# Attention's score, turn and value steps in other places, two more units turned by DMA, and two changes of order at norms

## The chip, the cores and the metric

The kernel runs on one core of one Trainium2 chip. The time is the device time of one execution in microseconds; the number that counts is the median of several runs. PE is the engine of the matmuls, DVE the vector engine, ACT the scalar engine, POOL the GpSimd engine, and SP the engine whose queue issues most DMAs.

## The reference

Two layers over 512 tokens of width 1024, all in float32. Each layer is a feed-forward block, a mixing block and a second feed-forward block; a norm ends the whole.

```python
for l in range(DEPTH):
    x = x + 0.5 * swiglu(rms_norm(x, ffn1_norm[l]), ffn1_wg[l], ffn1_wu[l], ffn1_wd[l])
    h = rms_norm(x, mix_norm[l])
    z = h @ w_in[l]            # q 512 | k 128 | v 128 | conv_B 512 | conv_C 512 | conv_h 512
    attn_out = sliding_window_attention(q, k, v, attn_sink[l])
    conv_out = short_conv(conv_B, conv_C, conv_h, conv_w[l])
    x = x + concat([attn_out, conv_out]) @ w_out[l]
    x = x + 0.5 * swiglu(rms_norm(x, ffn2_norm[l]), ffn2_wg[l], ffn2_wu[l], ffn2_wd[l])
return rms_norm(x, final_norm)
```

Attention has eight query heads of 64 and two key heads (four query heads share one). A block of 128 queries sees its own block of keys and the one before it, masked to a window of 128, with a bias that grows with the distance, and with one learned sink per head in the softmax:

```python
m = max(scores.max(-1), sink)
p = where(mask, exp(scores - m), 0)
probs = p / (p.sum(-1) + exp(sink - m))
out = probs @ v_band
```

## The kernel before, in words

**Products in two parts.** Every float32 product is made of three PE matmuls in a rounded format: high part of the weights by high and by low part of the data, and low part of the weights by high part of the data. So each tile of weights that arrives (`raw`) is split: ACT casts the high part (`wh`, line 222), DVE subtracts it from the raw tile for the low part (`wl`, line 223). `need_split` makes the splits in the order of the plan, `take_split` hands the next one to a group of matmuls and asks for the split three groups ahead. `need_raw` asks for the loads four units further ahead, from SP's queue; some units are sums of two tiles, and the second is added by an accumulating DMA from POOL's queue. Raw tiles live in a ring of eight buffers (`stock`), high and low parts in rings of four.

**Order of the work.** The program's order says what depends on what; a planner then places the instructions on each engine, by its own estimate of when each is ready, and sets the waits. `tc.issue_after(a)` (also `behind`) keeps later instructions of an engine behind instruction `a` on it, without waiting for its end. Inside `manual_schedule` regions PE keeps the order of the program.

**The mixing block** (`mix`). The norm's result comes as turned halves; `halves` makes the first three groups from them (keys, values, first pair of query heads), with weights that `hold` takes ahead. Then groups of 24 matmuls follow, one per 128 columns of `w_in`: j = 1 to 3 for the other query heads, then twelve for the convolution (two of C, two of h, two of B, twice). After each of them `attend(step)` issues a piece of attention; steps 3 to 5 follow the query groups j = 1 to 3 and 6 to 17 the twelve others. In this document the group before `attend(step)` is called group `step`.

**Attention by units.** A unit is one block of queries and one key head with its four query heads: unit number 4 g + n for block n and key head g. Blocks n = 0 have one block of keys, the others two. Each unit has these pieces, and each piece has a table that gives the step for each of the eight units:

- `scores`: matmuls of scores, then DVE adds the bias and takes the maximum, ACT takes the exponentials (line 1565), DVE divides. The probabilities `p` lie in a buffer of the raw ring.
- the turn, which the values need with keys across partitions. Either on PE (`turn`): up to eight transposes of 128x128 (line 1623), then a cast on ACT and a subtraction on DVE for each block of keys (lines 1626, 1627). Or by DMA, for the units with an entry in `SEND_AT`: `apart` (called at the end of `scores`) copies the two 16-bit halves of each number into two planes with two ACT copies (line 1588), `send` turns each plane with one transposing DMA from SP's queue (line 1595), `join` puts the halves together again with two ACT copies (line 1608), and casts and subtracts as the other way does (lines 1612, 1614).
- `values`: matmuls of the turned probabilities with the values (lines 1638, 1639), a copy on ACT and two additions on DVE.

A join of `JOIN_AT` is issued in `attend` itself; one of `LATE_JOIN_AT` after the split that follows it in `go_on`.

**Norms behind closing groups.** In `share` with `after`, the last products of a block end in the residual stream `x`; `after` is the next norm. Its squares are taken on ACT as parts of `x` are ready, its factor is found by a first guess on ACT (`guess`, line 650) and a Newton step on DVE (lines 649 to 661), and the scaled tiles `xn` are turned on PE (line 685). Of a turned tile, ACT casts the high part, and `rest` (DVE subtraction for the low part, line 697) and `keep` (a full copy on ACT, line 701; nothing at a mixing norm) are collected in `later` and issued by `go_on`, each behind the instruction that is named beside it. `added` is the last addition to `x`, `first` the second scaled tile.

Of the kernel before, what the change touches and what calls it, by code (L numbers as in the profile page):

```python
# [16 lines left out]
P = 128  # L17
# [25 lines left out]
EARLY = ("a11", "a12", "s3", "s2", "a22", "s1", "s4")  # L43
SCORES_AT = (5, 6, 7, 8, 9, 10, 12, 13)
TURN_AT = (6, None, 8, None, 11, None, 14, 15)
SEND_AT = (None, 7, None, 9, None, 11, None, None)
JOIN_AT = (None, None, None, None, None, 14, None, None)
LATE_JOIN_AT = (None, 10, None, 12, None, None, None, None)
VALUES_AT = (7, 11, 9, 13, 12, 15, 15, 16)
WARM = 3  # L50
# [26 lines left out]
def trunk_kernel(  # L77
# [252 lines left out]
    def hold(norm, n):  # L330

        first = state["group"]
        if norm.added:
            for ahead, one in ((2, norm.added), (3, norm.first)):
                with behind(one):
                    need_split(first + ahead)
        return [take_split(SPLIT_AHEAD - j)[1:] for j in range(n)]

# [243 lines left out]
    class Norm:  # L582
# [40 lines left out]
        def __call__(self, t, o):  # L623

            self.squared = nc.scalar.activation(
                junk(f"sq_{self.i}_{t}_{o}"),
# [52 lines left out]
        def turn(self, t, o, xn):  # L679
# [23 lines left out]
            if self.later is None:  # L703
                rest()
                keep()
            elif o:
                self.later.extend(((rest, "added"), (keep, "squared")))
            else:
                rest()
                self.later.append((keep, "squared"))  # L710

# [240 lines left out]
    def share(  # L952
# [6 lines left out]
        for step, (acc, operand, start) in enumerate(chains):  # L959
# [9 lines left out]
            for h in range(2):  # L969
# [11 lines left out]
                for o, t, sign in shares[step]:  # L981
                    for m in range(2):
# [7 lines left out]
                        if after and step == 6 and m:  # L990
                            after.added = added
                            after.go_on()
            if not soon:
# [493 lines left out]
    def mix(l, norm, after):  # L1487
# [36 lines left out]
        class Unit:  # L1524
# [52 lines left out]
            def apart(self):  # L1577

                if n_of(self) % NT == 1:
                    self.room = g8(f"pr_{self.name}", U16, (P, 4, KC * P))  # L1580
                else:
                    self.room = xpool.tile(
                        [P, 4, KC * P], U16, tag="xf", bufs=8, name=f"pr_{self.name}"
                    )
                src = self.p.bitcast(U16).rearrange("p h (b k z) -> p z h b k", b=2, z=2)
                with tc.issue_after(state["cast"].ins):
                    for z in range(2):
                        nc.scalar.copy(
                            self.room[:, z].rearrange("p (b h k) -> p h b k", b=2, h=4), src[:, z]
                        )  # L1590

            def send(self):
                with tc.issue_after(state["load"].ins):
                    for z in range(2):
                        nc.sync.dma_start_transpose(
                            self.room[:, 2 + z].rearrange("p (g q) -> p g q", q=P), self.room[:, z]
                        )

            def join(self):

                dst = self.p.bitcast(U16).rearrange("p h (k z) -> p z (h k)", z=2)
                turned = self.p.rearrange("p h k -> p (h k)").rearrange(
                    "p (b h q) -> p b h q", b=2, h=4
                )
                self.pt = []
                with tc.issue_after(state["cast"].ins):
                    for z in range(2):
                        nc.scalar.copy(dst[:, z], self.room[:, 2 + z])
                for kb in range(2):
# [39 lines left out]

        def n_of(unit):  # L1650
            return NT * unit.g + unit.n

        def attend(step, what=(VALUES_AT, JOIN_AT, TURN_AT, SEND_AT, SCORES_AT)):

# [29 lines left out]
        def go_on():  # L1684
# [4 lines left out]
            with tc.issue_after(last.ins) if last else nullcontext():  # L1689
                need_split(state["group"] - 1 + SPLIT_AHEAD)  # L1690
            attend(step - 1, (LATE_JOIN_AT,))

# [75 lines left out]
```

## Time and profile before

| what | value |
|---|---|
| median of 3 runs | 1641.26 us (1640.89 to 1641.5) |
| profiled execution | 1641.66 us |
| its span, first to last instruction | 1639.9 us |
| mean granted PE clock | 0.999 |
| PE transposes `pt` of attention | 64, both layers |
| transposing DMAs of attention | 12, both layers |

All times in rows are of this one profiled execution, in microseconds from the start of its span. A matmul's row shows how long it was under way; PE starts the next one before it ends, so the distance between starts tells what an instruction costs PE. A row of busy time counts overlapping instructions once. "Idle before" is time in which that engine had nothing under way, with what ended it.

### The profile page before, as it was taken

How to read it: one execution, taken by the hardware profiler on the slowest of the kernel's cores; microseconds unless marked ns; L12 is line 12 of the kernel's file. 1: busy time of each engine (PE TensorE's matmuls, PEld its weight loads, DVE VectorE, ACT ScalarE, POOL GpSimd, SP SyncE). 2: the span in 40 equal slices, each digit the busy share in tenths (PEclk: the TensorE clock that was granted, in tenths of full speed). 3: DMA queues.
4: the chain of work that ended last, by engine and by line, in shares of the span. 5: the costliest groups of instructions: out<-in, count | busy, mean ns of one | idle time of the engine just before them, and what ended most of it. 6: DMA issues, size and time to landing. Idle time of an engine off the chain costs nothing.

```text
span 1639.9 us, 21080 instructions
## 1 busy us (share of the span) xinstructions
PE 1629.8 (99%) x7576; PEld 1356.7 (83%) x7576; DVE 1300.8 (79%) x1718; ACT 1128.7 (69%) x1581; POOL 193.5 (12%) x172
## 2 busy tenths in 40 slices
PE   9999999999999999999999999999999999999998
PEld 7888888888888888888888888888988888888886
DVE  7987779877799867798788677896578987768895
ACT  7457777556867667786576777865587775777864
POOL 0011111100111111112001111110002101111111
PEclk9999999999999999999999999999999999999999
DMA  9379999932685788999837898996137857999991
GB/s 257 86 196 219 225 215 256 221 93 58 167 205 129 205 205 206 218 228 248 231 78 204 207 218 220 232 250 194 53 90 167 208 131 191 213 224 223 227 263 65
DMA packets 286844, 308.64 MB, mean 188 GB/s; under 512 B 108532, under 2 KB 171028, under 8 KB 286740
## 3 DMA queue, kind: packets, MB, share of 16 engines
q1 hardware_dynamic: 244212, 227.99, 47.8%
q0 software_dynamic: 41824, 78.65, 28.1%
q8 instruction: 59, 0.97, 0.2%
q10 hardware_dynamic: 704, 0.66, 0.1%
q14 instruction: 45, 0.37, 0.1%
HBM read 263.74 MB, written 2.10 MB: 162 GB/s over the span
## 4 chain that ended last, share of the span: by engine, by line
PE 92%; DVE 4%; ACT 1%; DMA 1%; issue 1%; SPq 0%; ACTq 0%; DVEq 0%
PE x L941 25%; PE y L941 13%; PE x_s L941 10%; PE w L941 6%; PE y_s L941 5%; PE down L373 3%; PE acc L314 3%; PE acc L315 3%; PE acc L317 3%; PE up L1097 3%; PE w_s L941 3%; PE acc L350 2%; DVE wl L223 1%; PE acc L839 1%; DMA raw<-in_w_out_dram 1%
## 5 line engine op out<-in xcount | busy, mean ns | idle before, releaser
L223 DVE TENSOR_TENSOR wl<-raw,wh 128x1024 fp32r<-128x1024 f32 (+1 forms) x493 | 596.2, 1214 | 219.9 <-ACT wh L222 216.7
L222 ACT CAST wh<-raw 128x1024 fp32r<-128x1024 f32 (+1 forms) x493 | 513.2, 1046 | 312.2 <-PE y L941 41.6
L941 PE MATMUL y<-wh,ft 128*128 128x512 f32 x608 | 187.3, 389 | 0.0
L941 PE MATMUL x<-wh,fb 128*128 128x512 f32 x608 | 187.3, 389 | 0.0
L941 PE MATMUL x<-wh,ft 128*128 128x512 f32 x608 | 187.3, 389 | 0.0
L941 PEld LDWEIGHTS x<-wh,ft 128*128 128x128 f32 x608 | 114.1, 188 | 23.7
L941 PEld LDWEIGHTS x<-wh,fb 128*128 128x128 f32 x608 | 114.1, 188 | 23.7
L941 PEld LDWEIGHTS y<-wh,ft 128*128 128x128 f32 x608 | 114.1, 188 | 23.7
L941 PE MATMUL y<-wl,ft 128*128 128x512 f32 x304 | 118.3, 389 | 0.0
L941 PE MATMUL x<-wl,fb 128*128 128x512 f32 x304 | 118.3, 389 | 0.0
L941 PE MATMUL x<-wl,ft 128*128 128x512 f32 x304 | 118.3, 389 | 0.0
L217 POOL DMA_DIRECT2D raw<-in_ffn_wu_dram x39 | 47.3, 1222 | 544.3 <-DMA raw<-in_ffn_wu_dram 327.0
L1266 ACT COPY raw_a<-pt 128x1024 uint16<-128x1024 uint16 x76 | 103.2, 1358 | 11.1 <-DMA pt<-pl 11.1
L314 PE MATMUL acc<-hh,wh 128*128 128x512 f32 x240 | 94.7, 394 | 0.0
L315 PE MATMUL acc<-hl,wh 128*128 128x512 f32 x240 | 93.8, 391 | 0.0
L317 PE MATMUL acc<-hh,wl 128*128 128x512 f32 x240 | 93.7, 391 | 0.0
L941 PE MATMUL w<-wh,fb 128*128 128x512 f32 x304 | 93.6, 389 | 0.0
L941 PE MATMUL x_s<-wh,ft_s 128*128 128x512 f32 x256 | 78.8, 389 | 0.0
L941 PE MATMUL y_s<-wh,ft_s 128*128 128x512 f32 x256 | 78.8, 389 | 0.0
L250 DVE TENSOR_TENSOR raw<-raw,raw 128x1024 f32<-128x1024 f32 x58 | 70.6, 1222 | 7.1 <-DMA raw<-in_ffn_wd_dram 5.9
L217 POOL DMA_DIRECT2D raw<-in_ffn_wg_dram x39 | 47.1, 1212 | 233.7 <-DVE u L1250 62.3
L941 PE MATMUL x_s<-wh,fb_s 128*128 128x512 f32 x240 | 73.9, 389 | 0.0
(364 smaller groups left out, 3421.3 us busy)
## 6 DMA issues: line engine op xcount, KB each, us to landing
raw<-in_ffn_wu_dram SPq DMA_DIRECT2D x120, 512.0 KB, 5.2
raw<-in_ffn_wd_dram SPq DMA_DIRECT2D x104, 512.0 KB, 6.3
raw<-in_ffn_wg_dram SPq DMA_DIRECT2D x80, 512.0 KB, 4.9
raw<-in_ffn_wu_dram POOLq DMA_DIRECT2D x39, 512.0 KB, 8.1
raw<-in_ffn_wg_dram POOLq DMA_DIRECT2D x39, 512.0 KB, 6.0
raw<-in_w_in_dram SPq DMA_DIRECT2D x36, 512.0 KB, 4.3
raw<-in_ffn_wd_dram POOLq DMA_DIRECT2D x32, 512.0 KB, 8.5
raw<-raw POOLq DMA_DIRECT2D x20, 512.0 KB, 8.5
```

The lines of the kernel that those rows point to most:

```text
L217: nc.gpsimd.dma_start(out=r, in_=rows_of(*more), accum_op=ALU.add)
L222: cast = nc.scalar.copy(hi, raw)
L223: state["sub"] = eng.tensor_sub(lo, raw, f32(hi))
L250: nc.vector.tensor_add(a11, a11, s1)
L314: nc.tensor.matmul(acc, hi[:, k, :], rhs[k][0], start=k == first, stop=False)
L315: nc.tensor.matmul(acc, hi[:, k, :], rhs[k][1], start=False, stop=False)
L317: nc.tensor.matmul(acc, lo[:, k, :], rhs[k][0], start=False, stop=k == last)
L350: nc.tensor.matmul(accs[j][:, t * H : (t + 1) * H], w[:, k, :], x_, start=t + k + i == 0, stop=k == KC - 1 and i == 2, skip_group_check=True,)
L373: nc.tensor.matmul(acc, a[:, k, tok], w[:, k, :], start=i + k + n == 0 and fresh[t], stop=i == last and k == 1 and n == 2, skip_group_chec ...
L941: nc.tensor.matmul(accs[u], x_[:, 2 * h + k, tok], w[:, k, :], start=start and h + k + i == 0, stop=h + k == 2 and i == 2, skip_group_chec ...
L1097: nc.tensor.matmul(accs[t], x_[:, tok], w[:, k, :], start=j + k + i == 0, stop=j == 3 and k == 1 and i == 2,)
L1266: nc.scalar.copy(room.rearrange("p c (n z) -> p c z n", z=2)[:, :, z, :], turned[0][:, NT * z + 2 * c : NT * z + 2 * c + 2, :],)
```

## The change

The tables of steps get new entries. Units 1, 2, 3, 5 and 6 go by DMA (before 1, 3 and 5), all with their join after the following split; unit 0's scores are issued in step 3 (before 5); values fall in steps 6 and 10 to 16, one unit each. The transposing DMAs now write into the buffer of `p` itself and the join into the planes; the planes of units 1 and 2 share one tile of the `g8` ring, those of units 3 and 5 one of the `xf` ring, and unit 6 takes a buffer of the raw ring.

At the mixing norm after a share (only layer 0 has one) `go_on` is called in `hold`, behind the split of the third held group, instead of at the end of `share`. At the norms after attention `keep` is queued behind `guess` instead of the last square.

```diff
--- before.py
+++ after.py
@@ -41,12 +41,11 @@
 LAST = INNER[:-1] + (("d", (9, 10)),)
 FORMS = ("a11", "a12", "s2", "s3", "s1", "a22", "s4")
 EARLY = ("a11", "a12", "s3", "s2", "a22", "s1", "s4")
-SCORES_AT = (5, 6, 7, 8, 9, 10, 12, 13)
-TURN_AT = (6, None, 8, None, 11, None, 14, 15)
-SEND_AT = (None, 7, None, 9, None, 11, None, None)
-JOIN_AT = (None, None, None, None, None, 14, None, None)
-LATE_JOIN_AT = (None, 10, None, 12, None, None, None, None)
-VALUES_AT = (7, 11, 9, 13, 12, 15, 15, 16)
+SCORES_AT = (3, 4, 5, 6, 10, 8, 9, 12)
+TURN_AT = (4, None, None, None, 11, None, None, 14)
+SEND_AT = (None, 5, 6, 7, None, 9, 10, None)
+JOIN_AT = (None, 8, 9, 10, None, 12, 13, None)
+VALUES_AT = (6, 10, 11, 12, 13, 14, 15, 16)
 WARM = 3
 XT_TAGS = ("sc", "aux", "aux", "mm", "sc", "sc", "aux", "aux")
 
@@ -334,6 +333,9 @@
             for ahead, one in ((2, norm.added), (3, norm.first)):
                 with behind(one):
                     need_split(first + ahead)
+                if norm.later is not None:
+                    norm.added = state["sub"]
+                    norm.go_on()
         return [take_split(SPLIT_AHEAD - j)[1:] for j in range(n)]
 
     def halves(norm, n, done):
@@ -622,7 +624,7 @@
 
         def __call__(self, t, o):
 
-            self.squared = nc.scalar.activation(
+            nc.scalar.activation(
                 junk(f"sq_{self.i}_{t}_{o}"),
                 xt(t, o),
                 AF.Square,
@@ -704,10 +706,10 @@
                 rest()
                 keep()
             elif o:
-                self.later.extend(((rest, "added"), (keep, "squared")))
+                self.later.extend(((rest, "added"), (keep, "guess")))
             else:
                 rest()
-                self.later.append((keep, "squared"))
+                self.later.append((keep, "guess"))
 
         def go_on(self):
 
@@ -989,7 +991,8 @@
                             after(2 * t + m, o)
                         if after and step == 6 and m:
                             after.added = added
-                            after.go_on()
+                            if not after.mixing:
+                                after.go_on()
             if not soon:
                 ops.make(*[chains[n][1] for n in {1: (4,), 2: (6, 5)}.get(step, ())])
             if between:
@@ -1576,36 +1579,32 @@
 
             def apart(self):
 
-                if n_of(self) % NT == 1:
-                    self.room = g8(f"pr_{self.name}", U16, (P, 4, KC * P))
-                else:
-                    self.room = xpool.tile(
-                        [P, 4, KC * P], U16, tag="xf", bufs=8, name=f"pr_{self.name}"
-                    )
                 src = self.p.bitcast(U16).rearrange("p h (b k z) -> p z h b k", b=2, z=2)
+                self.planes = rooms.pop(0)()
                 with tc.issue_after(state["cast"].ins):
                     for z in range(2):
                         nc.scalar.copy(
-                            self.room[:, z].rearrange("p (b h k) -> p h b k", b=2, h=4), src[:, z]
+                            self.planes[:, z].rearrange("p (b h k) -> p h b k", b=2, h=4), src[:, z]
                         )
 
             def send(self):
+                self.back = self.p.rearrange("p h k -> p (h k)").bitcast(U16)
+                self.back = self.back.rearrange("p (z n) -> p z n", z=2)
                 with tc.issue_after(state["load"].ins):
                     for z in range(2):
                         nc.sync.dma_start_transpose(
-                            self.room[:, 2 + z].rearrange("p (g q) -> p g q", q=P), self.room[:, z]
+                            self.back[:, z].rearrange("p (g q) -> p g q", q=P), self.planes[:, z]
                         )
 
             def join(self):
 
-                dst = self.p.bitcast(U16).rearrange("p h (k z) -> p z (h k)", z=2)
-                turned = self.p.rearrange("p h k -> p (h k)").rearrange(
-                    "p (b h q) -> p b h q", b=2, h=4
-                )
+                whole_ = self.planes.rearrange("p z n -> p (z n)")
+                dst = whole_.rearrange("p (n z) -> p z n", z=2)
+                turned = whole_.bitcast(F32).rearrange("p (b h q) -> p b h q", b=2, h=4)
                 self.pt = []
                 with tc.issue_after(state["cast"].ins):
                     for z in range(2):
-                        nc.scalar.copy(dst[:, z], self.room[:, 2 + z])
+                        nc.scalar.copy(dst[:, z], self.back[:, z])
                 for kb in range(2):
                     hi = g2(f"ph_{self.name}_{kb}", F32R, (P, 4, P))
                     lo = g2(f"pl_{self.name}_{kb}", F32R, (P, 4, P))
@@ -1647,10 +1646,26 @@
 
         todo = [Unit(n, g) for g in range(NKV) for n in range(NT)]
 
-        def n_of(unit):
-            return NT * unit.g + unit.n
-
-        def attend(step, what=(VALUES_AT, JOIN_AT, TURN_AT, SEND_AT, SCORES_AT)):
+        shared_rooms = {}
+
+        def half_of(name, half, make):
+            def room():
+                if not half:
+                    shared_rooms[name] = make(name)
+                return shared_rooms[name][:, half]
+            return room
+
+        def in_g8(name):
+            return g8(name, U16, (P, 2, 2, KC * P))
+
+        def in_xf(name):
+            return xpool.tile([P, 2, 2, KC * P], U16, tag="xf", bufs=8, name=name)
+
+        rooms = [half_of(f"pr_{l}_0", h, in_g8) for h in range(2)]
+        rooms += [half_of(f"pr_{l}_1", h, in_xf) for h in range(2)]
+        rooms.append(lambda: stock(f"pr_{l}_2", U16, (P, 2, KC * P)))
+
+        def attend(step, what=(VALUES_AT, TURN_AT, SEND_AT, SCORES_AT)):
 
             stages = {VALUES_AT: "values", TURN_AT: "turn", SEND_AT: "send", SCORES_AT: "scores"}
             done = None
@@ -1688,7 +1703,7 @@
             step += 1
             with tc.issue_after(last.ins) if last else nullcontext():
                 need_split(state["group"] - 1 + SPLIT_AHEAD)
-            attend(step - 1, (LATE_JOIN_AT,))
+            attend(step - 1, (JOIN_AT,))
 
         for pair in range(2):
             cs = []
```

## The prediction, made before the changed kernel was run

> **What bounds the kernel now.** I read the page first, then the waits of PE, then busy time by stretch around attention, then the order of time on each engine where something is edited.
>
> ```profile
> span 1639.9 us, 21080 instructions
> ...
> PE 1629.8 (99%) x7576; PEld 1356.7 (83%) x7576; DVE 1300.8 (79%) x1718; ACT 1128.7 (69%) x1581; POOL 193.5 (12%) x172
> ```
>
> ```profile
> PE idle L151 <- DVE warm L785: 1.2, 1, 1.2
> PE xt L685 <- DVE xn L661: 0.8, 2, 0.4
> PE acc L350 <- DVE wl L223: 0.5, 1, 0.5
> PE y_m L941 <- ACT wh L222: 0.3, 1, 0.3
> ```
>
> PE is busy for all but 10.1 us (1639.9 less 1629.8), and its listed waits come to 2.8 us. So the end is set by how much PE has to do. There are two ways to gain: take instructions off PE, or remove one of these few waits. Everything else only has to stay hidden. The wait at the start (L151) is not touched; the other three lie near the edits. The next rows are the attention stage of layer 0 (layer 1 repeats it).
>
> ```profile
> core 0: us, PE busy (x) PEld busy (x) DVE busy (x) ACT busy (x) POOL busy (x), PEclk, DMA share, GB/s
> 370.00:390.00 20.00, 20.00 (x104) 16.73 (x103) 13.51 (x41) 12.79 (x31) 0.00 (x0) 1.00 0.10 27
> 390.00:410.00 20.00, 20.00 (x103) 16.81 (x102) 16.69 (x54) 15.49 (x33) 2.32 (x2) 1.00 0.32 80
> 410.00:430.00 20.00, 20.00 (x99) 16.80 (x99) 15.09 (x45) 19.63 (x38) 0.26 (x1) 1.00 0.64 154
> 430.00:450.00 20.00, 20.00 (x101) 16.76 (x100) 14.90 (x39) 15.04 (x36) 4.65 (x4) 1.00 0.69 168
> 450.00:470.00 20.00, 19.95 (x88) 16.18 (x88) 19.77 (x24) 11.27 (x13) 6.16 (x6) 1.00 0.91 174
> ```
>
> PE never stops here. ACT is full for 20 us (19.63) and PE does not feel it; DVE is full from 450 on (19.77).
>
> **Part 1: two more units turned by DMA.** Before, units 1, 3 and 5 of the eight go by DMA; now 1, 2, 3, 5 and 6. Units 2 and 6 each have two blocks of keys of four heads: eight PE transposes each.
>
> ```profile
> 397.22 0.39 PE L317 MATMUL acc<-hh,wl 128*128 128x512 f32 x1
> 397.45 0.40 PE L314 MATMUL acc<-hh,wh 128*128 128x512 f32 x1
> 397.68 1.13 PE L1623 MATMUL pt<-ident,p 128*128 128x128 f32 x8
> 398.56 0.48 PE L315 MATMUL acc<-hl,wh 128*128 128x512 f32 x1
> 398.88 0.40 PE L317 MATMUL acc<-hh,wl 128*128 128x512 f32 x1
> ```
>
> What counts is the distance between starts, since PE overlaps its instructions. Eight transposes hold PE from 397.68 to 398.56: 0.88 us, 0.11 each. The group they interrupt then takes 0.32 us for one matmul (398.56 to 398.88) instead of 0.23 (397.22 to 397.45): 0.09 more. So a unit costs PE 0.97 us, and two units in two layers are **-3.9 us**. The Trainium skill ("TensorE: Matmul & The Clock Gate", Part 4: PE-mode transpose) gives about 275 ns for a transpose inside a kernel; at that price the 32 would be an estimated 8.8 us and the whole sum near -10. The row's distance decides against it.
>
> What the DMA way adds goes to ACT and SP:
>
> ```profile
> L1565 ACT ACTIVATE p<-p,nm 128x256 f32<-128x256 f32 (+1 forms) x32 | 15.1, 475 | 3.5 <-DVE nm L1559 3.5
> L222 ACT CAST wh<-raw 128x1024 fp32r<-128x1024 f32 x13 | 13.7, 1052 | 9.4 <-PE acc L315 9.4
> L1608 ACT COPY p<-pr 128x1024 uint16<-128x1024 uint16 x6 | 7.9, 1361 | 0.0
> L1588 ACT COPY pr<-p 128x1024 uint16<-128x1024 uint16 x6 | 6.0, 1045 | 0.0
> L1612 ACT CAST ph<-p 128x512 fp32r<-128x512 f32 x6 | 3.5, 622 | 0.0
> ```
>
> Six copies of each kind are three units, so one unit takes 2.0 us to part (L1588) and 2.6 us to join (L1608): 4.6, two units 9.3 us of ACT per layer. The two casts and two subtractions of a unit stay. From 370 to 450 ACT is busy 12.79 + 15.49 + 19.63 + 15.04 = 62.95 of 80 us; with the rest it is 72 of some 78. It fits, since the first scores come two groups earlier, into the 7.2 us that ACT has free before 390. I put it at **0 on the path**, hidden by PE's groups; the second rival below is that cover gone. New tiles change no shape: the copies read and write as many elements as before. Two units now share one tile by halves; if the planner took the halves for one, ACT would wait for one landing, at most 3.3 us by the next rows, in a stage where a late cast has more room than that. I take 0.
>
> ```profile
> L1595 SPq DMA_TRANSPOSE pr<-pr x12: 1243/1264/1325, 392.2 to 1232.7; - x12
> ...
> DMA to landing us min/median/max: 3.2/3.2/3.3
> ```
>
> ```profile
> 384.31 0.37 SPq L206 DMA_DIRECT2D raw<-in_w_in_dram  x1
> 392.25 2.63 SPq L1595 DMA_TRANSPOSE pr<-pr  x2
> 394.98 0.52 SPq L206 DMA_DIRECT2D raw<-in_w_in_dram  x1
> ```
>
> SP issues two more pairs per layer, 2.6 us each. A send waits on SP for the copies, and the loads of weights queue behind it: here nothing is issued for 7.6 us before 392.25, and the load follows at 394.98. PE waits for nothing in that stretch, as loads are asked for four units, some 25 us, ahead. The new tables put sends into five of the six groups 5 to 10, so such a hold-up comes oftener but no longer; 0. DMA has room (share 0.10 to 0.69 until 450). POOL's accumulating loads keep their order.
>
> Slots: a unit's probabilities lie in the ring of eight buffers for raw weights. At the fullest (groups 9 and 10) five are now taken, four of units and one by unit 6's planes, against four before. Three are left for weights, and each group uses up one. Towards the end they come free earlier, because a unit lets its buffer go at its join. 0 net.
>
> **Part 2: values spread, last turn a group earlier.** Unit 7 is turned in group 14 instead of 15 while its values stay in 16.
>
> ```profile
> 452.53 0.39 PE L1638 MATMUL o<-ph,vv 128*128 128x512 f32 x1
> 452.99 0.39 PE L1638 MATMUL o<-ph,vv 128*128 128x512 f32 x1
> 453.43 0.50 PE L1639 MATMUL o<-pl,vv 128*128 128x512 f32 x1
> ```
>
> Two values matmuls are 0.46 apart from L1638 to L1638, 0.23 each, but the last L1639 starts 0.44 after its L1638: PE waits 0.21 us for the subtraction. With a group more between turn and use that goes, in both layers: **-0.4 us**. DMA units now have a whole group between join and values, so I see nothing late behind it.
>
> **Part 3: the norm before attention in layer 0.** The third held group's low part is now subtracted before the norm's own two subtractions.
>
> ```profile
> 341.86 0.28 PE L350 MATMUL acc<-hh,wh 128*128 128x256 f32 x1
> 341.98 0.28 PE L350 MATMUL acc<-hl,wh 128*128 128x256 f32 x1
> 342.78 0.39 PE L350 MATMUL acc<-hh,wl 128*128 128x256 f32 x1 [0.52 <-DVE wl L223]
> ```
>
> ```profile
> 340.04 1.29 DVE L697 TENSOR_TENSOR hl<-xt,hh 128x512 fp32r<-128x512 f32 x2
> 341.51 1.22 DVE L223 TENSOR_TENSOR wl<-raw,wh 128x1024 fp32r<-128x1024 f32 x1
> ```
>
> The matmul that needs wl starts 0.80 us after the one before it, where 0.12 is the distance (341.86 to 341.98); PE loses 0.68. In the new order wl runs from 340.04 to 341.26, before PE asks for it at 342.1, and hl ends near 342.5. The matmul at 342.1 is the third of twelve in the first half of the third group, and hl is first read in the second halves, ten matmuls later: 343.3. So next in line is hl, with 0.8 us to spare. I take **-0.6 us**, a little less than the whole, since the restarted group may keep a few hundredths of it. The other three norms do not pass here: only this one is a mixing norm that comes from a share.
>
> **Part 4: full copies queued behind the guess** at the norms after attention (both layers).
>
> ```profile
> 502.66 1.05 ACT L701 COPY hf<-xt 128x512 f32<-128x512 f32 x2
> 503.60 0.30 ACT L650 ACTIVATE r<-v,eps 128x2 f32<-128x2 f32 x1
> ```
>
> ```profile
> 502.87 0.16 DVE L649 TENSOR_TENSOR v<-ss 128x2 f32<-128x2 f32 x1
> 502.94 1.23 DVE L223 TENSOR_TENSOR wl<-raw,wh 128x1024 fp32r<-128x1024 f32 x1
> 504.07 0.17 DVE L653 TENSOR_SCALAR v<-v 128x2 f32<-128x2 f32 x1
> ```
>
> The guess could start near 503.1 instead of 503.6. But DVE, which must finish the factor, has meanwhile begun a weight split and holds until 504.07, after the guess ended (503.90). An earlier guess helps only if the planner puts the factor ahead of that split. Bounds: 0, and the wait of 0.4 us per layer that the list of waits shows; if the split then comes too late for its group, it costs up to its 1.2. I take **0**, the nearest to the row.
>
> **Sum.** -3.9 - 0.4 - 0.6 = -4.9. Against it I set 0.2 for scores of early units that now cut into a group, two or so at 0.09 (bounds 0 and 0.7, eight insertions). That is -4.7 on the profiled execution, which took 1641.66 (span 1639.9 and 1.8 around it), 0.4 above the median 1641.26: on the median, **1636.5 us**. Its own range, from the bounds above, is 1635 to 1638.
>
> **The rivals.**
> *The split moves too.* If Part 4's wait goes as well, that is the 0.8 of the list of waits: 1635.7. For it: r then comes half a microsecond earlier. Against: while DVE waits for r it is idle, and takes a split that is ready, as it did here.
>
> *ACT falls behind (slower).* Groups 8 to 10 now hold three scores, two partings and three joins. By the rows: the exponentials 1.9 a unit (15.1 over eight), so 5.7; partings 4.0; joins 7.9 and their six casts 3.5; three weight casts 3.2: 24.3 us, and conv's copies beside them. A group is 24 matmuls at 0.23 and eight matmuls of scores at about half that, some 6.5 us; three give 19.5. ACT comes out 5 us late, say 7 with conv's. A high part wh is cast when its slot falls free (9.4 us of ACT's idle time end with PE's acc), three groups or 20 us ahead of its use, so 7 us late is still in time, and the full stretch 410 to 430 cost PE nothing. It decides from where a cast or a join comes later than its lead: joins have two groups, 13 us, less their own 4. If the last two joins of the crowd come 3 us too late each, that is 6 us per layer, 12 in all: 1648. For it: ACT runs in order, and a join in front of a cast holds it.
>
> *Given back to DVE.* From 450 DVE is full, and PE would come to W_out 2 us earlier per layer. If DVE starts no earlier, PE waits there for what it saved: up to 4.2 of the 4.7 returns, 1640.8. For it: 19.77 of 20. Against: DVE has 5.1 us free in 430 to 450, and turn and values of the last units move there.
>
> *The turn by DMA is the wrong tool.* If data came later than its join, units 2 and 6 would hold PE. From the rows: two issues and 3.2 to landing end 4.6 us after the send, and the join is three groups, 20 us, later. It decides only if a pair takes over four times as long; one microsecond beyond, four times, gives back 4: 1640.5. The Trainium skill ("VectorE: DVE Perf Modes", Rules for kernel authors) says to transpose 128x128 on TensorE when PSUM will do, and its table of transpose paths has 1309 ns per block by DMA; sixteen blocks would be an estimated 21 us per unit. The trace does not agree: both planes land in under 5.
>
> **How the numbers follow.** Forecast 0.58, split moved 0.12, DVE 0.12, turn late 0.02, ACT late 0.16. About 0.2%, 3.3 us, is what a measurement of this kernel tells from no change. The first two are faster by more: 0.70; the two give-backs fall within it: 0.14; ACT late is slower: 0.16. The range runs from 1634.3 (everything gained, Part 4 at its best) to 1642, past both give-backs; it leaves out ACT late and little else.
>
> **What would show it.** Right: 32 transposes pt instead of 64, 20 DMA transposes and 20 copies of each kind instead of 12; the waits on L350 and on pl gone; first exponentials of attention some 12 us earlier; span near 1635; the wait on xn still there. Wrong: PE waiting for wh or ph between 400 and 450 (ACT late), or a new wait in W_out's chains after 455 for wl or a form (DVE). A span under 1634 would mean that transposes cost PE more than the distance of their starts.

## The result and the profile after

| | median us | range, runs | ratio to the kernel before on the same chip |
|---|---|---|---|
| before | 1641.38 | 1640.72 to 1643.06, 8 | |
| changed | 1645.99 | 1644.05 to 1649.15, 8 | 1.0029 [1.0018, 1.0040] |

The forecast was 1636.5 and faster; the changed kernel is slower by 0.29%. Its profiled execution took 1644.05 us and is the fastest of the eight, so the profile shows 2.4 us of loss (1644.05 less 1641.66) and the medians 4.6.

The page of the changed kernel, its span and busy time:

```profile
span 1642.2 us, 21053 instructions
...
PE 1627.6 (99%) x7544; PEld 1354.0 (82%) x7544; DVE 1301.3 (79%) x1718; ACT 1144.0 (70%) x1597; POOL 195.9 (12%) x172
```

PE has 32 instructions fewer, as the change says, and is busy 2.2 us less (1629.8 before). But it is idle for 14.6 us of the span (1642.2 less 1627.6) where it was idle for 10.1: 4.5 more. Minus 2.2 plus 4.5 is the 2.3 by which the span grew. Its waits tell where the idle time is:

```profile
PE pt L1622 <- DVE p L1576: 4.9, 2, 2.5
PE idle L150 <- DVE warm L787: 1.2, 1, 1.2
PE xt L687 <- DVE xn L663: 0.8, 2, 0.4
PE y_m L943 <- ACT wh L221: 0.2, 1, 0.2
PE sc L1547 <- DVE q L1687: 0.2, 1, 0.2
```

The first line is new: twice, once per layer, PE stands still for 2.5 us before a transpose `pt`, until DVE has written the probabilities `p`. The wait on L350 (0.5) is gone, the one for `xn` stands as it was, a small one for the queries `q` is new. 4.9 + 0.2 - 0.5 - 0.1 is the 4.5.

Busy time by stretch, in the columns of before (PE, PEld, DVE, ACT, POOL, PEclk, DMA share, GB/s):

```profile
370.00:390.00 20.00, 19.96 (x103) 16.65 (x102) 16.64 (x58) 15.91 (x43) 0.00 (x0) 1.00 0.23 42
390.00:410.00 20.00, 20.00 (x98) 16.83 (x97) 15.87 (x43) 19.98 (x34) 2.67 (x2) 1.00 0.53 117
410.00:430.00 20.00, 17.56 (x87) 14.47 (x86) 14.70 (x39) 19.86 (x39) 1.88 (x1) 1.00 0.67 161
430.00:450.00 20.00, 20.00 (x94) 16.62 (x93) 15.15 (x33) 14.38 (x27) 4.92 (x4) 1.00 0.82 210
450.00:470.00 20.00, 20.00 (x90) 16.57 (x89) 15.27 (x20) 10.73 (x12) 5.59 (x5) 1.00 0.79 147
```

PE loses its 2.44 us in 410 to 430; ACT is now full for 40 us on end, 390 to 430, where it was full for 20.

**Whose turn it is.** The transposes are those of unit 4 (first block, second key head), whose turn stays on PE in step 11. PE's order of time in the changed kernel, from that unit's scores to its turn:

```profile
410.85 0.22 PE L1547 MATMUL sc<-k,q 128*128 128x128 f32 x1
...
419.06 0.39 PE L314 MATMUL acc<-hl,wh 128*128 128x512 f32 x1
421.89 0.33 PE L1622 MATMUL pt<-ident,p 128*128 128x128 f32 x1 [2.44 <-DVE p L1576]
...
423.81 0.39 PE L316 MATMUL acc<-hh,wl 128*128 128x512 f32 x1
```

and in the kernel before:

```profile
404.11 0.22 PE L1544 MATMUL sc<-k,q 128*128 128x128 f32 x1
...
417.83 0.60 PE L1623 MATMUL pt<-ident,p 128*128 128x128 f32 x4
```

Before, PE came to the turn 13.7 us after the scores began (417.83 less 404.11). The new tables put unit 4's scores into step 10 (before 9) and leave the turn in 11, so PE comes 8.4 us after (at 419.06 plus the usual 0.23). The turn starts at 421.89, 2.6 us late, and the same again in layer 1: 5.2 us. What lies between is DVE's order in the changed kernel:

```profile
413.09 0.16 DVE L1572 TENSOR_TENSOR sums<-sums,es 128x4 f32<-128x4 f32 x1 [1.76 <-ACT es L1571]
...
415.47 0.85 DVE L1643 TENSOR_TENSOR m<-o,ol 64x256 f32<-64x256 f32 x2 [0.23 <-ACT ol L1640]
416.34 0.35 DVE L1551 CUSTOM_DVE_ANT_0 p<-sc,bias,sink 128x128 f32<-128x128 f32 x1
...
420.22 0.17 DVE L1572 TENSOR_TENSOR sums<-sums,es 128x4 f32<-128x4 f32 x1 [1.70 <-ACT es L1571]
...
421.55 0.88 DVE L1576 TENSOR_SCALAR p<-p,sums 128x128 f32<-128x128 f32 x4
```

and ACT's:

```profile
415.34 1.99 ACT L1586 COPY pr<-p 128x1024 uint16<-128x1024 uint16 x2
417.24 1.35 ACT L1607 COPY pr<-p 128x1024 uint16<-128x1024 uint16 x1
418.46 0.39 ACT L1568 ACTIVATE p<-p,nm 128x128 f32<-128x128 f32 x1
```

The last of the scores matmuls ends at 411.9; DVE takes their maxima only from 416.34, since its queue first waits twice for ACT, for another unit's sums (1.76) and its copied values (0.23). ACT comes to the exponentials at 418.46, behind a parting and a join of DMA units. DVE writes `p` from 421.55: 10.7 us after the scores began. Before, the same way took 9.8 us:

```profile
405.40 0.35 DVE L1548 CUSTOM_DVE_ANT_0 p<-sc,bias,sink 128x128 f32<-128x128 f32 x1
...
413.89 0.87 DVE L1573 TENSOR_SCALAR p<-p,sums 128x128 f32<-128x128 f32 x4
```

So the way was hardly longer; it lost a group of cover.

### The profile page after: what moved, and what is told of

It is laid out like the page before. It is cut to its first block, busy times and chain, and to the rows that moved or that the text cites. A ratio compares the mean times of both kernels' runs of the same rounds, so it can differ in the third digit from the quotient of the medians.

```text
span 1642.2 us, 21053 instructions
## 1 busy us (share of the span) xinstructions
PE 1627.6 (99%) x7544; PEld 1354.0 (82%) x7544; DVE 1301.3 (79%) x1718; ACT 1144.0 (70%) x1597; POOL 195.9 (12%) x172
## 4 chain that ended last, share of the span: by engine, by line
PE 90%; ACT 5%; DVE 4%; issue 1%; DMA 0%; ACTq 0%; DVEq 0%
PE x L943 25%; PE y L943 13%; PE x_s L943 10%; PE w L943 6%; PE y_s L943 5%; PE down L375 3%; PE up L1100 3%; PE w_s L943 3%; PE acc L313 2%; PE acc L314 2%; PE acc L316 2%; PE acc L352 2%; DVE wl L222 1%; ACT p L1568 1%; ACT pr L1586 1%
```

## The experiments

Theory A: the loss is unit 4's turn, which has one group between it and its scores. Theory B: ACT, full with five DMA units, is late for PE wherever the turn stands. Each heading's time is a median, with the ratio to the kernel before on its chip; that kernel had medians of 1642.2 to 1642.6 in these comparisons.

**The changed kernel again, unedited: 1645.51, ratio 1.0024 [1.0013, 1.0034].**

> The changed kernel once more, unedited, for the distance between its profiled execution (1644.05, the fastest of eight) and its median (1645.99). Theory: the two waits of PE for unit 4's probabilities (2.4 us each) are at times long enough that PE's clock drops behind them; then slower executions show a mean clock of 0.997 to 0.998, and a profile of one shows a stretch at half clock right behind such a wait. Rival: the wait itself differs from execution to execution, as transfers do; then the clock stays at 0.999 and the wait in a slower execution is longer than 2.5 us. Both: median 1645 to 1647, and the two waits at the transposes of unit 4 are there again.

The waits were the same: 4.9, 2, 2.5. This execution took 1645.43, 1.4 more than the first one, and one stretch by windows and PE's order behind the first wait say why:

```profile
421.90:425.30 3.40, 3.40 (x11) 2.72 (x10) 2.75 (x7) 3.38 (x6) 0.00 (x0) 0.50 0.74 215
```

```profile
421.63 0.33 PE L1622 MATMUL pt<-ident,p 128*128 128x128 f32 x1 [2.45 <-DVE p L1576]
...
424.92 0.57 PE L316 MATMUL acc<-hh,wl 128*128 128x512 f32 x1
425.33 0.40 PE L313 MATMUL acc<-hh,wh 128*128 128x512 f32 x1
```

The granted clock was 0.50 for 3.4 us. The same instructions, from the turn's first transpose to the tenth behind it, took 3.29 us (421.63 to 424.92) and in the first profile 1.92 (421.89 to 423.81); with the next one the loss is 1.5. The second wait of this execution, and both of the first, were not followed by it. So a wait costs its 2.6 us and sometimes 1.5 more, which goes towards the medians' being above the first profile. How often it struck, the mean granted clock of each execution tells roughly: such a stretch lowers the mean by 0.001 (half of 3.4 us in 1644). It was 0.998 in this execution and 0.999 in the first profile; it was 0.998 or less in 17 of 20 executions of the changed kernel, in 5 of 35 of the kernel before beside the second measurement, and in 2 of 12 and none of 12 of the next two kernels, which have no such wait.

**Only the turn of unit 4 a step later: 1641.32, ratio 0.9988 [0.9978, 0.9998].**

```diff
-TURN_AT = (4, None, None, None, 11, None, None, 14)
+TURN_AT = (4, None, None, None, 12, None, None, 14)
```

> One entry of the changed kernel: unit 4 is turned in step 12 instead of 11, nothing else. Theory (ACT is behind by the work of the joins and partings, and PE, whose order is fixed beforehand, stands before unit 4's transposes): the turn comes a group of 5.4 us later, more than the 2.4 us that it waited, so both waits go, about 4.9 to 5.2 us in all: 1638.5 to 1640.5, below the kernel before. Since no long idle of PE is left, executions lie within 2 us of each other. Rival (the ring of raw buffers or the transfers are what is short, and unit 4 only shows it): the wait moves to another place, the time stays above 1643.

The wait at `pt` is gone. The way from scores (412.03) to `p` (422.70) is as long as in the changed kernel, 10.7 us, and PE comes to the turn at 425.68. The time missed the forecast of 1638.5 to 1640.5, and the executions lie 4.1 us apart, not 2. The span fell by 2.8 us (1642.2 to 1639.4) and not by 5.2, as other waits are longer in this profile: 0.6 at the first loads and 1.3 in the feed-forward blocks, at 265 and at 1583.

```profile
PE x_s L943 <- DVE wl L222: 1.3, 2, 0.9
```

The one at 265, 0.9 of it, lies ahead of every edit, and three other kernels of this document show 0.3 to 0.9 at the same place; so it is no wait that the edit has moved.

**Only the scores of unit 4 sooner: 1640.22, ratio 0.9983 [0.9973, 0.9993].**

```diff
-SCORES_AT = (3, 4, 5, 6, 10, 8, 9, 12)
+SCORES_AT = (3, 4, 5, 6, 7, 8, 9, 12)
```

> One entry of the changed kernel: unit 4's scores come in step 7, which had none, instead of 10; its turn stays in 11. Theory: its exponentials pass ACT before the crowd of groups 8 to 10, the probabilities are ready long before PE's transposes, both waits go: 1638.5 to 1640.5. ACT has as much to do as before, so some other piece may be a few tenths late. Rival (what is short is the ring of raw buffers): unit 4 now holds a buffer four groups longer, six of eight are taken at the fullest, and loads of weights come too late: PE waits for wh or wl, time above 1644.

The wait is gone here too, and ACT is as full as in the changed kernel. Its stretches:

```profile
390.00:410.00 20.00, 20.00 (x101) 16.97 (x100) 15.39 (x51) 19.98 (x40) 1.68 (x1) 1.00 0.55 127
410.00:430.00 20.00, 20.00 (x96) 16.68 (x95) 13.99 (x31) 19.93 (x32) 1.30 (x1) 1.00 0.58 141
```

PE is busy for all of both. A full ACT alone costs PE nothing, so theory B in its plain form falls: one entry of a table turns 0.24% slower into 0.17% faster.

**The kernel before with the two norm reorderings alone: 1641.48, ratio 0.9992 [0.9984, 1.0000].**

> The kernel before with the two changes of order at the norms and nothing of attention. By the steps of the prediction: the wait for wl behind the closing group of layer 0 goes (0.6 to 0.7 us), the waits for xn at the norms after attention stay (0.4 us each, since DVE is in a weight split when the guess is ready): 1640.7. Rival: the earlier guess takes the xn waits away too: 1639.5. Second rival: something else comes late behind the norms and the loss of the whole change lies here: above 1643.

The wait on L350 is gone and the one for `xn` stays at 0.8, 2, 0.4. The measurement holds the 0.6 us that the prediction gave it, and can't tell it from nothing.

**Four units by DMA, unit 6 on PE again: 1646.51, ratio 1.0027 [1.0017, 1.0037].**

```diff
-TURN_AT = (4, None, None, None, 11, None, None, 14)
-SEND_AT = (None, 5, 6, 7, None, 9, 10, None)
-JOIN_AT = (None, 8, 9, 10, None, 12, 13, None)
+TURN_AT = (4, None, None, None, 11, None, 13, 14)
+SEND_AT = (None, 5, 6, 7, None, 9, None, None)
+JOIN_AT = (None, 8, 9, 10, None, 12, None, None)
```

> The changed kernel with unit 6 back on PE (turned in step 13, no send, no join); unit 4 stays at scores 10 and turn 11. Theory (ACT full): unit 6's parting (2.0 us on ACT) no longer stands before unit 4's exponentials, so its probabilities come about 2 us sooner and most of the 2.4 us of waiting goes in each layer; eight transposes per layer come back, 0.97 us each layer on PE. Together 2 x (2.0 to 2.4) gained and 1.9 lost: span 1642.2 less 2.1 to 2.9, time 1641 to 1642. Rival (ACT is not what makes unit 4 late): the two waits stay at 2.4 us and the time rises by 1.9, to 1646 to 1648.

I had thought that ACT would come to unit 4's exponentials sooner without unit 6's copies. That failed, and the time is the rival's: the wait list has 4.6, 2, 2.3, and ACT's order shows what took their place.

```profile
415.99 1.35 ACT L1607 COPY pr<-p 128x1024 uint16<-128x1024 uint16 x1
417.21 1.04 ACT L221 CAST wh<-raw 128x1024 fp32r<-128x1024 f32 x1
418.15 0.61 ACT L1611 CAST ph<-pr 128x512 fp32r<-128x512 f32 x1
418.67 0.40 ACT L1568 ACTIVATE p<-p,nm 128x128 f32<-128x128 f32 x1
```

The copies of the parting are gone, a cast of weights and one of a join stand in front instead, and the exponentials start at 418.67 as against 418.46.

**The second parting copy on POOL: 1643.56, ratio 1.0006 [0.9997, 1.0015].**

```diff
-                    for z in range(2):
-                        nc.scalar.copy(
-                            self.planes[:, z].rearrange("p (b h k) -> p h b k", b=2, h=4), src[:, z]
-                        )
+                    for z, put in enumerate((nc.scalar.copy, nc.gpsimd.tensor_copy)):
+                        put(self.planes[:, z].rearrange("p (b h k) -> p h b k", b=2, h=4), src[:, z])
```

> The changed kernel with its own tables; of the two copies that part a unit, the second is made by POOL, which is nearly idle in attention, instead of ACT. ACT has 0.95 us less for each of the five units per layer, four of them before unit 4's exponentials. Theory (ACT's queue): unit 4's probabilities come up to 3.8 us sooner, the two waits of PE go or fall below 0.5 us: 1639 to 1641. Rival (the tables leave the turn of unit 4 too close whatever ACT has to do, or the ring of raw buffers is short): the waits stay above 2 us, time 1644 or more. A side effect could be POOL's copy being slow (several us) and sharing SBUF with DVE: then sends come later, with 3 groups to spare.

The wait shrank to 2.9, 2, 1.4, but not because `p` came sooner. It came from 422.38; PE reached the turn later, since the planner had put it six matmuls further on (PE stood still from 421.1, not from 419.3). ACT's exponentials began at 420.20 and waited for DVE's `nm` for 0.50. Less work on ACT, here as with four units, did not bring `p` sooner. Both forecasts missed: the waits and the time lie between them.

**Three DMA units as before, unit 4's scores a step later: 1646.51, ratio 1.0018 [1.0009, 1.0027].**

```diff
-SCORES_AT = (5, 6, 7, 8, 9, 10, 12, 13)
+SCORES_AT = (5, 6, 7, 8, 10, 9, 12, 13)
```

> The kernel before, with three units by DMA, in which only the steps of scores of units 4 and 5 change places: unit 4 in step 10 (was 9), unit 5 in step 9 (was 10); unit 4's turn stays in step 11. Theory of the distance: from unit 4's scores on PE to its p take about 10 us on DVE and ACT, one group gives 6.5, so PE must stand still at pt in both layers though only three units go by DMA: a wait of 1 to 3.5 us at each, +2 to +6 us, 1644 to 1647. Rival, that the crowd of five units on ACT is needed: no wait at pt above 0.3 us, within 1 us of the kernel before.

This puts the one shift into the kernel before. Two of its waits:

```profile
PE o L1638 <- ACT ph L1612: 1.6, 2, 0.8
...
PE pt L1623 <- DVE p L1573: 0.8, 2, 0.4
```

It is slower by 3 us by the ratio and 4.0 by the medians, as the theory's time had it, but its waits were missed: 0.4 at `pt` and not 1 to 3.5, and 0.8 beside it at values of unit 1 for a high part `ph`. These two are 2.4 of the 3.7 us between the spans (1643.6 and 1639.9); 0.9 more is a wait at 265, ahead of the edit. The way from scores to `p` took only 6.5 us here (411.45 to 417.96), and PE came to the turn 6.4 after the scores. In the changed kernel PE came after 8.4, in time for such a way; it waited since the way took 10.7. So one group of distance is enough to bring a wait with three units too, but its size there belongs to the long way, and what makes that is only partly settled: it was 9.8 and 6.5 with three units, 10.3 with four and 10.7 with five, so the order in which DVE and ACT take their work seems to count at least as much as how much of it there is.

**Everything early a step later, unit 4's turn in 12: 1640.86, ratio 0.9993 [0.9984, 1.0001].**

```diff
-SCORES_AT = (3, 4, 5, 6, 10, 8, 9, 12)
-TURN_AT = (4, None, None, None, 11, None, None, 14)
-SEND_AT = (None, 5, 6, 7, None, 9, 10, None)
-JOIN_AT = (None, 8, 9, 10, None, 12, 13, None)
-VALUES_AT = (6, 10, 11, 12, 13, 14, 15, 16)
+SCORES_AT = (4, 5, 6, 7, 10, 8, 9, 12)
+TURN_AT = (5, None, None, None, 12, None, None, 14)
+SEND_AT = (None, 6, 7, 8, None, 9, 10, None)
+JOIN_AT = (None, 9, 10, 11, None, 12, 13, None)
+VALUES_AT = (7, 11, 12, 13, 13, 14, 15, 16)
```

> The changed kernel with every early step of the tables one group later except unit 4's scores (scores 4, 5, 6, 7, 10, 8, 9, 12; turns 5, 12, 14; sends 6, 7, 8, 9, 10; joins 9, 10, 11, 12, 13; values 7, 11, 12, 13, 13, 14, 15, 16). Theory: no wait at pt, since unit 4 has two groups between scores and turn, and no early scores that wait for their queries: 1638 to 1640, at or a little below the kernel with only unit 4's scores sooner. Rival, that the late start lets ACT fall behind: waits at pt, pl or wh in groups 10 to 14 and 1641 or more.

The rival's wait came (3.0, 2, 1.5 at `pt`), though two groups lie between; the time lies between both forecasts. DVE's row at the maxima of unit 4:

```profile
417.85 0.35 DVE L1551 CUSTOM_DVE_ANT_0 p<-sc,bias,sink 128x128 f32<-128x128 f32 x1 [1.21 <-ACT pr L1607]
```

The scores were ready at 410.3, and DVE's last wait before the maxima is for a join's copy on ACT. That copy reads another unit's buffer of the ring, which then comes free for this unit's `p`. With joins a step later the way from scores to `p` took 15.0 us (409.3 to 424.3). So a kernel can lose here by the ring as well, though the changed one shows no such wait.

**Unit 0's scores out of the query groups.** First with unit 4's scores in step 7 and unit 0's beside unit 1's in step 4: **1640.30, ratio 0.9989 [0.9980, 0.9998].**

```diff
-SCORES_AT = (3, 4, 5, 6, 10, 8, 9, 12)
-TURN_AT = (4, None, None, None, 11, None, None, 14)
-VALUES_AT = (6, 10, 11, 12, 13, 14, 15, 16)
+SCORES_AT = (4, 4, 5, 6, 7, 8, 9, 12)
+TURN_AT = (5, None, None, None, 11, None, None, 14)
+VALUES_AT = (7, 10, 11, 12, 13, 14, 15, 16)
```

> The kernel with unit 4's scores in step 7, and now unit 0 a step later in everything (scores 4, turn 5, values 7). Theory: with unit 0 in step 3 its scores cut into a group and wait for q four times (0.2, 0.3, 0.15 us and slow restarts), its turn and its first values cut in as well (0.2 to 0.3 us each); per layer about 1 us of this goes, and nothing that PE needs moves: 1638 to 1639, 1 to 2 us below the kernel with unit 4's scores sooner (1640.2). Rival: the early start is what keeps ACT ahead, and units 0 and 1 in one step put it behind again: waits at some pt or pl of 1 us or more, 1641 or above.

It gained nothing against unit 4's scores sooner (1640.22, on another chip): the second unit of the step waits until DVE has taken the maxima of the first.

```profile
PE sc L1547 <- DVE mx L1551: 1.6, 2, 0.8
```

Then one unit in each step from 4 to 10, the joins as in the changed kernel: **1638.84, ratio 0.9979 [0.9970, 0.9988]**, and on another chip 1639.12, ratio 0.9982 [0.9973, 0.9991]. Its median is the lowest of all, and both intervals lie below 1.

```diff
-SCORES_AT = (3, 4, 5, 6, 10, 8, 9, 12)
-TURN_AT = (4, None, None, None, 11, None, None, 14)
-SEND_AT = (None, 5, 6, 7, None, 9, 10, None)
-VALUES_AT = (6, 10, 11, 12, 13, 14, 15, 16)
+SCORES_AT = (4, 5, 6, 7, 8, 9, 10, 12)
+TURN_AT = (5, None, None, None, 11, None, None, 14)
+SEND_AT = (None, 6, 7, 8, None, 10, 11, None)
+VALUES_AT = (7, 10, 11, 12, 13, 14, 15, 16)
```

> The changed kernel with one unit's scores in each of steps 4 to 10 and unit 7's in 12 (scores 4, 5, 6, 7, 8, 9, 10, 12; sends 6, 7, 8, 10, 11; turn of unit 0 in 5 and its values in 7; joins, the other turns and the other values as in the changed kernel). My account of the early scores: they wait for nothing once they come a step after their queries are formed, and unit 4 has three groups before its turn; so no waits at pt, sc or o between 360 and 470, some 1 to 2 us per program below the kernel with only unit 4's scores sooner: 1638 to 1639.5, a span near 1636.5. Rival, that a wait only changes its place each time the tables move (as when the first two units shared a step): a new wait of 0.5 us or more in 360 to 470, at pt, pl, ph or sc, and 1640 or more.

> The kernel with five units and one unit's scores per step, unedited, beside the one with three units on the same chip: 1638 to 1640 and a ratio of 0.997 to 0.999. If the theory of Part 1's price holds, its median lies 3.5 to 4.3 us below that of the kernel with three units; if the rival holds, less than 1.5.

Its page and its waits:

```profile
span 1637.0 us, 21061 instructions
...
PE 1624.8 (99%) x7544; PEld 1353.1 (83%) x7544; DVE 1301.9 (80%) x1718; ACT 1142.6 (70%) x1597; POOL 192.1 (12%) x172
```

```profile
PE xt L806 <- DMA x<-in_x_dram: 1.2, 1, 1.2
PE idle L150 <- DVE warm L787: 1.2, 1, 1.2
PE y_m L943 <- ACT wh L221: 1.1, 2, 0.7
PE xt L687 <- DVE xn L663: 0.8, 2, 0.4
PE o L1638 <- DVE pl L1613: 0.7, 2, 0.4
```

None at `pt` or `sc`; a small one at values (0.35 per layer) that I had said would not be there. The time held.

**The same with units 2 and 6 on PE: 1640.11, ratio 0.9988 [0.9979, 0.9997].** This is the price of the DMA turn by itself, on the chip of the second of the two runs above.

```diff
-TURN_AT = (5, None, None, None, 11, None, None, 14)
-SEND_AT = (None, 6, 7, 8, None, 10, 11, None)
-JOIN_AT = (None, 8, 9, 10, None, 12, 13, None)
+TURN_AT = (5, None, 9, None, 11, None, 13, 14)
+SEND_AT = (None, 6, None, 8, None, 10, None, None)
+JOIN_AT = (None, 8, None, 10, None, 12, None, None)
```

> The kernel with one unit's scores per step (scores 4 to 10 and 12), but with units 2 and 6 turned on PE again (turns 5, 9, 11, 13, 14; sends 6, 8, 10; joins 8, 10, 12), so that three units go by DMA as before: the price of the DMA turn by itself, in tables without a wait at pt. Theory of the prediction's Part 1, 0.11 us per transpose and 0.09 per restart: two units by eight transposes in two layers are worth 3.9 us, so this span is 3.5 to 4.3 above that of the kernel with five units (1637.0), near 1641, the time 1642 to 1643, and PE makes 7576 matmuls. Rival, that most of what the transposes cost is hidden or that the gain of the DMA turn came from the order alone: a span within 1.5 us of 1637.0.

The rival was right: the spans differ by under 1.5 us, and the medians by less than the 3.5 to 4.3 of the theory. Its page:

```profile
span 1637.4 us, 21097 instructions
...
PE 1627.6 (99%) x7576; PEld 1356.8 (83%) x7576; DVE 1300.0 (79%) x1718; ACT 1127.7 (69%) x1581; POOL 192.0 (12%) x172
```

Two more units by DMA take 2.8 us off PE's busy time (1627.6 to 1624.8), but the spans differ by 0.4 and the medians by 1.0 (1640.11 to 1639.12). The rest comes back as waits. The kernel with three units has none of its own at `o`, 0.2 at `y_m` and 0.5 at the first loads; against the list above that is 0.7 + 0.9 + 0.7 = 2.3. The 0.7 at the first loads lies ahead of all edits and differs from execution to execution (not listed before, 1.2 here), so 1.6 of the 2.8 are given back behind the turns. Profiles of the five-unit kernel vary by as much as the rest: its execution on this chip had PE busy for 1625.3 us, 1.5 at `y_m` and a span of 1637.8, above the one with three units. So PE's busy time falls by 2.3 to 2.8 us, and what is left of it is near the medians' 1.0, which the two intervals (0.9973 to 0.9991, 0.9979 to 0.9997) don't tell from nothing. The wait at `y_m` is for a cast on ACT, whose queue there starts with a load of `w_out`. With five units:

```profile
471.60 1.06 ACT L221 CAST wh<-raw 128x1024 fp32r<-128x1024 f32 x1 [1.81 <-DMA raw<-in_w_out_dram]
```

and with three:

```profile
471.73 1.05 ACT L221 CAST wh<-raw 128x1024 fp32r<-128x1024 f32 x1 [1.57 <-DMA raw<-in_w_out_dram]
```

The load lands at nearly the same time in both, and ACT works from it without a stop to the cast that PE waits for (478.15 and 478.28); PE comes sooner and waits longer. What sets the time of the load was not followed up.

## Why the prediction was wrong

- **The step that failed is in Part 1: "0 on the path"** for ACT's 9.3 us per layer, "hidden by PE's groups". The cover was reckoned for casts and joins, in whole stretches of ACT's time, and not for the turn that stays on PE. The diff itself moves unit 4's scores from 9 to 10 against a turn in 11; the second rival counts this unit's exponentials among ACT's work, but no sentence of the prediction asks whether its turn still finds `p` ready, so that entry was put at nothing without a reason. It is worth 5.2 us in the profile (two times 2.6), and one group more before the turn is worth 4.2 in the medians (1645.51 to 1641.32), three groups more 5.3 (to 1640.22).
- **Part 1's -3.9 was too large too.** The distance of starts gave 0.97 a unit; by busy time the four (two units in two layers) are worth 2.3 to 2.8, and in time about 1.0, because waits behind it take back the rest. That is a give-back like the third rival's, and 0.9 of it comes in `w_out`'s stage as it said, but behind a load and ACT, not on DVE; 0.7 comes at values behind joins.
- **The +0.2 for early scores was too small.** Unit 0's eight matmuls in the changed kernel lie at three places among those of the query groups, and PE comes to some before the queries. Its order of time from the first of them, at one of them, and behind the last:

```profile
363.29 0.22 PE L1547 MATMUL sc<-k,q 128*128 128x128 f32 x1
...
365.81 0.39 PE L316 MATMUL acc<-hh,wl 128*128 128x512 f32 x1
366.34 0.33 PE L1547 MATMUL sc<-k,q 128*128 128x128 f32 x1
...
368.28 0.39 PE L316 MATMUL acc<-hh,wl 128*128 128x512 f32 x1
```

  At this one PE takes 0.53 instead of 0.23. From the first row to the last are 4.99 us, in which PE starts eight scores matmuls and 14 of the group's; at 0.114 and 0.227 each, as where nothing waits, they take 4.1. So unit 0 costs 0.9 us, and 0.9 in layer 1 as well: 1.8 against the 0.2, and above its bound of 0.7. The kernel with one unit per step has none of this (eight scores and one matmul of the group take 1.14 there, 368.58 to 369.72), and its median is 1.4 below the one with only unit 4's scores sooner (1638.84 and 1640.22, on two chips, with intervals that overlap).
- **The three sizes together** are 5.2 for the turn, 1.6 for the early scores and 1.1 to 1.6 for Part 1: about 8. The profiled execution missed its forecast by 7.1 (1644.05 less 1637.0, which is 1641.66 less 4.7); the terms overlap or vary by the rest.
- **Parts 2, 3 and 4 came as worked out.** The values of the last unit no longer wait (their matmuls start 0.23 apart), and L350's wait is gone, as `wl` is now subtracted from 339.88. The `xn` wait stays at 0.4 per layer. By themselves the norm reorderings are within the measurement's reach of the -0.6.
- **The rival that ended slower had the sign and, in part, the engine, not the place or the price.** It had ACT too late by joins and casts, "PE waiting for wh or ph", 6 us per layer. PE waited for `p`, 2.6 per layer, and ACT's load counts only together with the distance: ACT is as full with unit 4's scores sooner and costs nothing there, and the same shift with three units costs 0.4 at `pt` and 0.8 at values per layer.
- **What was right in direction** shows once the tables are mended: the change is then 3.0 to 3.5 us faster than before (0.9982 and 0.9979 of 1642), of which some 2.0 is there with three units too (0.9988).

## What to carry to other kernels

When a table of steps changes, go through it piece by piece and write down, for each consumer that stays in the bound engine's fixed order, the time from producer to consumer and the groups left between; here the way from scores to probabilities took 6.5 to 15.0 us and one group gave 6.4 to 8.4. Here an engine that was full cost nothing until such a consumer stood behind it, and moving one producer gained more than lightening the engine, since the planner filled the freed place with other work. A saving on the bound engine should be discounted by the next loads and casts, which may keep their own time: of 2.3 to 2.8 us of busy time saved, about 1.0 was left in the medians.

## What the runs showed of the hardware

- A gap of 2.45 us on PE was followed by 3.4 us at half the granted clock once; five other gaps of 2.3 to 2.5 us in three profiled executions were not. The same traces show what sets the one apart. In each of them the clock falls to 0.50 after PE's last work too. In the second execution of the changed kernel this fall (1640.44) comes 1218.55 us after the first (421.89), which is 357 times 3.4133 us, the length of the slow stretch. Counted back from the last fall in steps of 3.4133 us, the one gap (419.18 to 421.63) lies whole inside one step (418.48 to 421.89). In the three traces each of the other five gaps is cut by the end of a step, and at most 1.93 us of it lie in one. So whether such a gap costs the clock seems to depend on where it falls among these steps, as far as six gaps can show it. The Trainium skill ("TensorE: Matmul & The Clock Gate", Part 1) describes windows of about 3.4 us that run freely, with half rate after an idle one, and its rules ("Why this matters for your kernels") warn of idle gaps above some 3 us. The traces agree with the windows (3.4133); the gap of 2.45 us was shorter than the rule's.
- A copy of 128x1024 16-bit elements took POOL 1.03 to 2.01 us, 1.04 in the median of ten (the kernel with the second parting copy on POOL), against 1.04 on ACT.
